# Tile offsets in on-chip memory and an earlier split of the mixed tokens, in a one-layer hybrid decoder trunk

## The chip, the cores and the metric

The kernel runs on one core of a Trainium2 chip. The metric is the device time of one execution in microseconds (us); the time of a kernel is the median of its runs. Before the change it is 2625.88 us, the median of 3 runs (2619.48 to 2629.32 us). The profile is taken from one further execution.

## The reference

One layer of a decoder trunk on 2048 tokens of width 1024, in float32. Cut to what matters:

```
mod = silu(c) @ w_ada + b_ada                      # shift, scale, gate for both sub-layers
h = rms(x) * norm_mix * (1 + scale1) + shift1
z = h @ w_in                                       # 1024 -> 3736 columns
mixed = concat(gla(...), hgrn2(...), mlstm(...))   # token mixers, chunk by chunk along the sequence
x = x + gate1 * (mixed @ w_out)                    # 1024 -> 1024
h = rms(x) * norm_mlp * (1 + scale2) + shift2
ff = relu(h @ w_ff1)**2 @ w_ff2                    # 1024 -> 4096 -> 1024
x = x + gate2 * ff
return rms(x) * final_norm
```

The three mixers are causal, so the mixing of a stretch of tokens needs the state that the stretch before it left. The dense products (`w_in`, `w_out`, `w_ff1`, `w_ff2`) have no order among token stretches.

## The kernel before, in words

**Quarters.** The tokens are cut into four quarters of 512 (`TQ`). All in-projections run first, quarter after quarter (`inproj`); then, for each quarter, the output projection (`outproj`), and the FFN (`f1` for `w_ff1`, `f2` for `w_ff2`) in six blocks of 5, 6, 6, 6, 5 and 4 hidden tiles (`NF`; `LB` is the last block's number).

**Dense products in three passes.** A float32 operand is split into a high part, rounded to the type `fp32r`, and a low part that holds the rest (`split`: ScalarE casts the high part, VectorE subtracts to get the low one). A product is the sum of three passes, high with high, high with low, low with high (`PASSES`). So each output tile of 128 x 512 over 1024 inputs is 8 x 3 = 24 matmuls. All go through the helper `mm` (line 165); `weights` (line 198) loads and splits a weight tile. Matmuls of the mixers go through `mm_late` (line 180) and `tr_late` (line 184) in plain float32.

**Pools.** On-chip memory is filled from both ends. From the left: constants, and the pool `wp`, with the ring of 15 split activation tiles (`ht`, 4,096 bytes a partition), raw weights (`raw`), split weights (`wt`), work tiles (`m5`). From the right: `m1`, the mixers' tiles, some of them small. When all mixing is done, `m1` is closed and the pool `lp` takes its place for the last quarter: split mixed tokens (`mt`, in pairs), split FFN inputs (`h2_0` to `h2_7`, shown as `h`), raw tiles, and the last block's split `w_ff2` weights. Tile sizes are rounded up to 32 bytes. A pool's base follows from all that was allocated ahead of it.

**Operands.** In the in-projection of most column groups the activation is the stationary operand and 384, 408 or 512 weight columns stream (`part`, line 834); two slices of 128 input rows lie behind one another in a weight tile. The 408 columns are group `q`. In `outproj`, `f1` and `f2` the weights are stationary and 512 tokens stream; in `f2_last`, at the very end, 256 tokens.

**Order.** The order on each engine is planned ahead from program order: a piece under `ahead()` counts as some 60 instructions earlier. Slots of a ring go to its tiles in the order of their first writes. Mixing is fed in between dense products: `pump` (line 1117) is called after every few matmuls and spends credit on steps of the block passes (pairs of positions within 16 tokens, on VectorE) and of the mixing chunks (four for each quarter); `finish(q)` (line 1131) emits at once whatever is left of quarter q's mixing; `prog.hold` stops mixing steps, not block passes, while the mixers' buffers are lent out.

**Around the change.** At the end of a quarter's FFN, ahead of the last `f2`, the main loop calls `finish(q + 1)`, and `outproj_in` (line 928) loads quarter q + 1's mixed tokens from device memory into mixing tiles lent for it (`spare`: `X`, `tm`, `v`) by POOL's DMA queue and splits them into eight ring tiles. `outproj` sets `prog.hold`, and `ffn_in` clears it when the FFN inputs are made. In `f1` the product is followed by its evacuation under `ahead()`: ReLU, square (which first writes the hidden tile), square, subtraction. This happens at the end of quarters 0 and 1; the last quarter's output projection comes earlier, within quarter 2, from `lp`.

Of the kernel before, what the change touches and what calls it, by code (L numbers as in the profile page):

```python
# [14 lines left out]
P = 128  # L15
# [86 lines left out]
def trunk(ctx, tc, I, out):  # L102
# [19 lines left out]
        return pm[0].tile([P, 1024], F32, tag="psm", name=name)  # L122


    mpx, ipx = ExitStack(), ExitStack()
    mpool = lambda name, bufs: mpx.enter_context(tc.tile_pool(name=name, bufs=bufs, side="right"))
    m1 = mpool("m1", 1)
# [67 lines left out]

    nraw, raw3 = [0], [ipool]

    def weights(src, n, lp=None):

        with ahead():  # L200
            nraw[0] += 1
            if raw3 and nraw[0] % 3 == 0 and n <= 816:
                raw = raw3[0].tile([P, 816], F32, tag="raw3", name="raw", bufs=1)
            else:
                raw = wp.tile([P, 1024], F32, tag="raw", name="raw", bufs=2)
            r = raw[:, 0:n]
            dma(out=r, in_=src)
            wt = (lp or wp).tile([P, 2, 1024], F32R, tag="wt", name="wt", bufs=4 if lp else 3)
            split(wt[:, 0, 0:n], wt[:, 1, 0:n], r)
        return wt[:, :, 0:n]  # L210

    def ring():
        return wp.tile([P, 2, TQ], F32R, tag="ht", name="ht", bufs=15)
# [89 lines left out]
    SH = m1.tile([P, 3, 128], F32, name="SH")  # L303
    SG3 = m1.tile([P, 256], F32, name="SG3")
    SG4 = m1.tile([P, 128], F32, name="SG4")
    SC = m1.tile([P, 2, 130], F32, name="SC")
    zero = m1.tile([P, 384], mybir.dt.bfloat16, name="zero")
    vaug = m1.tile([P, 4, 65], F32, name="vaug")
    mcar = m1.tile([4, 1], F32, name="mcar")
    Sd = m1.tile([P, 784], F32, name="Sd")  # L310
    for t_ in (SH, SG3, SG4, SC, zero, mcar, Sd):
        G.memset(t_, 0.0)
# [31 lines left out]
    def gates(q):  # L344

        g = gm[q % 3]
        li, y = g[:, 0, :], g[:, 1, :]
        w = lambda n, c=128: m1.tile([P, c], F32, tag="g_" + n, name="g_" + n)
        al, mt, b, be, lf, sm = w("al"), w("mt", 129), w("b"), w("be"), w("lf"), w("sm", 6)
        last = A.activation(out=al, in_=y, func=AF.Abs)  # L350
        V.tensor_scalar(out=lf, in0=y, scalar1=0.0, scalar2=None, op0=ALU.min)
        with ln_exp(last):
            A.activation(out=al, in_=al, func=AF.Exp, scale=-1.0)
            last = A.activation(out=al, in_=al, func=AF.Ln, bias=1.0)
        V.tensor_tensor(out=lf, in0=lf, in1=al, op=ALU.subtract)
        V.tensor_tensor_scan(out=b, data0=ones, data1=lf, initial=0.0, op0=ALU.mult, op1=ALU.add)
        V.memset(mt, 0.0)
        for n in range(4):
            r = slice(32 * n, 32 * n + 4)
            V.tensor_copy(out=mt[r, 0:1], in_=mcar if n == 0 else mt[32 * n - 32:32 * n - 28, 128:129])  # L360
            V.tensor_tensor_scan(out=mt[r, 1:129], data0=lf[r, :], data1=li[r, :], initial=mt[r, 0:1],
                                 op0=ALU.add, op1=ALU.max)
        V.tensor_copy(out=mcar, in_=mt[96:100, 128:129])
        yield
        V.tensor_tensor(out=al, in0=b, in1=mt[:, 1:129], op=ALU.subtract)
        V.tensor_tensor(out=be, in0=li, in1=b, op=ALU.subtract)
        for n in range(4):
            dma_m(out=R.al[q][n], in_=al[32 * n:32 * n + 4, :])
        ps = pt("ps_g")
        burst()  # L370
        tr = lambda i, t: tr_late(out=ps[:, 128 * i:128 * i + 128], in_=t, identity=ident)
        tr(0, be)
        V.tensor_tensor(out=sm[:, 0:1], in0=b[:, 127:128], in1=mt[:, 128:129], op=ALU.subtract)
        V.tensor_tensor(out=sm[:, 1:2], in0=sm[:, 0:1], in1=mt[:, 0:1], op=ALU.add)
        with ln_exp(last):
            A.activation(out=al, in_=al, func=AF.Exp, bias=mt[:, 0:1])
            A.activation(out=b, in_=mt[:, 1:129], func=AF.Exp, scale=-1.0)
            A.activation(out=lf, in_=be, func=AF.Exp, bias=sm[:, 0:1])
            A.activation(out=sm[:, 1:2], in_=sm[:, 1:2], func=AF.Exp)
        V.tensor_scalar(out=lf, in0=lf, scalar1=0.125, scalar2=None, op0=ALU.mult)  # L380
        V.tensor_scalar(out=sm[:, 2:6], in0=cst[:, 648:652], scalar1=sm[:, 1:2], scalar2=None, op0=ALU.mult)
        yield
        burst()
        for i, t in ((1, al), (2, b), (3, lf)):
            tr(i, t)
        gT = m1.tile([P, 4, 4, 4], F32, tag="gT", name="gT", bufs=2)
        V.tensor_copy(out=gT, in_=ps.rearrange("p (i n x) -> p i n x", i=4, n=4)[:, :, :, 0:4])
        ps = pt("ps_sc")
        burst()
        for pr in range(2):  # L390
            mm_late(ps[:, 4 * pr:4 * pr + 4], cst[:, 392 + 128 * pr:520 + 128 * pr], sm[:, 2:6], True, True)
        sc = m1.tile([P, 2, 4], F32, tag="sc", name="sc", bufs=2)
        V.tensor_copy(out=sc, in_=ps[:, 0:8].rearrange("p (a c) -> p a c", a=2))
        R.gT, R.sc = gT, sc
        yield
# [30 lines left out]
    def chunk(q, n, L, N):  # L426
# [120 lines left out]
        with hold:  # L547
            for pr in range(2):
                mm_late(psx_[:, pr, 260:390], L.qk[:, pr, :], SC[:, pr, :], True, True)
            for h in range(4):  # L550
                mm_late(psv[:, 65 * h:65 * h + 65], pe[:, h, :], vaug[:, h, :], True, True)
        hi_ = m1.tile([P, 4, 65], F32, tag="hi_", name="hi_")
        V.tensor_tensor(out=hi_.rearrange("p (a h) c -> p a h c", a=2),
                        in0=psx_[:, :, 260:390].rearrange("p a (h c) -> p a h c", c=65),
                        in1=gT[1].rearrange("p (a h) -> p a h", a=2)[:, :, :, None].to_broadcast([P, 2, 2, 65]),
# [7 lines left out]
        yield  # L563
        nxt(load_qk)
        nxt(load_al)
        st = m1.tile([P, 56], F32, tag="st40", name="st40")
        den, mu, ss, rs = st[:, 0:4], st[:, 4:8], st[:, 8:24], st[:, 24:40]
        V.scalar_tensor_tensor(out=den, in0=hi_[:, :, 64], scalar=-1.0, in1=hi_[:, :, 64],
                               op0=ALU.mult, op1=ALU.max)
# [201 lines left out]
    def inproj(q, hts, nxt):  # L771
# [62 lines left out]
        def part(g, c0, n, ps, kk):  # L834

            kind = GROUPS[g][0]
            w = weights(I[f"wg{g}"][:, 2 * kk:2 * kk + 2, c0:c0 + n], 2 * n).rearrange("p a (k n) -> p a k n", k=2)
            for ti in range(len(ps)):
                for k2 in range(2):
                    k = 2 * kk + k2  # L840
# [87 lines left out]
    def outproj_in(q, lp=None):  # L928
        mt = []
        if lp is None:  # L930
            raws = spare(SPARE_Z, lambda c: R.zx[q][:, c, :])
        for c in range(KT):
            if lp is None:
                raw = raws[c]
# [54 lines left out]
                yield  # L989
        prog.hold = False  # L990

    def f1(h2, ft):
        w = weights(I["w1"][ft].rearrange("p c n -> p (c n)"), 1024)
        hd = ring()
        ps = psd.tile([P, 512], F32, tag="psd", name="ps_f1")
        for k in range(KT):
            for i, (a, b) in enumerate(PASSES):
                mm(ps, w[:, b, 128 * k:128 * k + 128], h2[k][:, a], k == 0 and i == 0, k == KT - 1 and i == 2)
            if k % 2:
                pump(1.3)  # L1000
        with ahead():
            r = m5()
            A.activation(out=r, in_=ps, func=AF.Relu)  # L1003
# [189 lines left out]
        pass  # L1193
    tail = iter(())
    for q in range(NQ):
        hds = []
        for ft in range(NF[0]):
            hds.append(f1(h2, ft))
            next(tail, None)
# [4 lines left out]
        for b in range(LB):  # L1204
# [5 lines left out]
            next(steps, None)  # L1210
            f2(hds, b, acc, steps)
            for i in range(1, NF[b + 1]):
                nh.append(f1(h2, F0[b + 1] + i))
                next(steps, None)
            hds = nh
            if q == NQ - 2 and b == EARLY:
                finish(NQ - 1)
                mpx.close()
                lp = ctx.enter_context(tc.tile_pool(name="lp", bufs=1, side="right"))
                sm1 = outproj(NQ - 1, outproj_in(NQ - 1, lp), lp)  # L1220
        if q == NQ - 1:
# [1 line left out]
            break  # L1223
        steps = iter(())
        if q < NQ - 2:
            finish(q + 1)
            h2n = []
            steps = ffn_in(h2n, q + 1, *outproj(q + 1, outproj_in(q + 1)))
        f2(hds, LB, acc, steps)
        h2 = h2n  # L1230
        tail = final_steps(q, acc)
# [34 lines left out]
```

## Time and profile before

| | |
|---|---|
| median of 3 runs | 2625.88 us (2619.48 to 2629.32) |
| profiled execution | 2632.36 us, span 2630.3 us |
| TensorE, matmuls | 2545.6 us busy, 97% |
| TensorE, weight loads | 2177.5 us, 83% |
| VectorE | 1787.1 us, 68% |
| ScalarE | 1232.5 us, 47% |
| GpSimd | 259.9 us, 10% |
| mean granted clock of TensorE | 0.989 |

How to read it: busy times are sums over the whole span and do not say which engine a stage waits for; for that, views by stage, by group and by wait are shown with the prediction. Each line names the engine, the source line, the operation, and the tiles as written <- read. PE is TensorE's matmuls, PEld its weight loads (they run beside the matmuls), DVE is VectorE, ACT ScalarE, POOL GpSimd, SP the queue that issues most DMAs. Matmuls are pipelined and their ends are modelled, so the distance between starts says more than a duration. The digits of tile names are left out: `h2_0` to `h2_7` appear as `h`, `ps_f1` and `ps_f2` both as `ps_f`.

### The profile page before, as it was taken

How to read it: one execution, taken by the hardware profiler on the slowest of the kernel's cores; microseconds unless marked ns; L12 is line 12 of the kernel's file. 1: busy time of each engine (PE TensorE's matmuls, PEld its weight loads, DVE VectorE, ACT ScalarE, POOL GpSimd, SP SyncE). 2: the span in 40 equal slices, each digit the busy share in tenths (PEclk: the TensorE clock that was granted, in tenths of full speed). 3: DMA queues.
4: the chain of work that ended last, by engine and by line, in shares of the span. 5: the costliest groups of instructions: out<-in, count | busy, mean ns of one | idle time of the engine just before them, and what ended most of it. 6: DMA issues, size and time to landing. Idle time of an engine off the chain costs nothing. (4 is left out here: it accounts for less than half of the span.)

```text
span 2630.3 us, 39618 instructions
## 1 busy us (share of the span) xinstructions
PE 2545.6 (97%) x15050; PEld 2177.5 (83%) x15050; DVE 1787.1 (68%) x3344; ACT 1232.5 (47%) x2191; POOL 259.9 (10%) x435
## 2 busy tenths in 40 slices
PE   5899999999999999999999999999999999999998
PEld 5889888899888788888878888888888888888887
DVE  8785786987975978876887666547566645533335
ACT  4654455545643634554453545445445543433333
POOL 0101102021102112112110000100000010000000
PEclk9999999999999999999999999999999999999999
DMA  8777676586457345446464343444433254433332
GB/s 266 211 222 218 180 216 189 170 243 198 144 143 234 107 113 146 138 142 166 128 184 135 125 131 116 146 133 161 131 123 119 88 181 148 141 114 93 94 96 80
DMA packets 160199, 401.75 MB, mean 153 GB/s; under 512 B 20473, under 2 KB 60490, under 8 KB 160010
## 3 DMA queue, kind: packets, MB, share of 16 engines
q1 hardware_dynamic: 129338, 306.51, 37.3%
q0 software_dynamic: 30672, 92.73, 12.7%
q8 instruction: 118, 1.93, 0.3%
q14 instruction: 71, 0.58, 0.1%
HBM read 336.21 MB, written 62.95 MB: 152 GB/s over the span
## 5 line engine op out<-in xcount | busy, mean ns | idle before, releaser
L165 PE MATMUL ps_f<-ht,wt 128*128 128x512 f32 (+1 forms) x5472 | 1252.3, 388 | 5.6 <-ACT ht L225 5.5
L165 PEld LDWEIGHTS ps_f<-ht,wt 128*128 128x128 f32 x5472 | 1008.8, 188 | 213.4 <-ACT ht L225 6.1
L194 DVE TENSOR_TENSOR wt<-raw,wt 128x1024 fp32r<-128x1024 f32 (+3 forms) x436 | 499.1, 1146 | 431.3 <-ACT wt L193 429.6
L193 ACT CAST wt<-raw 128x1024 fp32r<-128x1024 f32 (+3 forms) x436 | 431.6, 991 | 665.2 <-PE ps_f L165 345.4
L165 PE MATMUL ps_ip<-wt,ht 128*128 128x384 f32 (+2 forms) x3072 | 593.6, 352 | 29.4 <-ACT st L823 8.6
L165 PEld LDWEIGHTS ps_ip<-wt,ht 128*128 128x128 f32 x3072 | 554.6, 193 | 56.2 <-ACT st L823 10.6
L1023 DVE SCALAR_TENSOR_TENSOR acc<-ps_f,mod,acc 128x512 f32<-128x512 f32 (+1 forms) x200 | 145.1, 727 | 106.0 <-PE ps_f L165 105.3
L1003 ACT ACTIVATE m<-ps_f 128x512 f32<-128x512 f32 x128 | 76.9, 601 | 288.4 <-PE ps_f L165 288.2
L165 PE MATMUL ps_f<-h,wt 128*128 128x512 f32 x768 | 181.4, 397 | 0.0
L165 PEld LDWEIGHTS ps_f<-h,wt 128*128 128x128 f32 x768 | 144.6, 188 | 35.6 <-issue 0.5
L165 PE MATMUL ps_op<-ht,wt 128*128 128x512 f32 x576 | 133.1, 393 | 3.8 <-ACT ht L193 3.8
L165 PEld LDWEIGHTS ps_op<-ht,wt 128*128 128x128 f32 x576 | 109.0, 190 | 26.9 <-ACT ht L193 3.9
L323 POOL DMA_DIRECT2D blk<-zq x144 | 93.6, 661 | 353.0 <-DVE prod L333 169.4
L333 DVE TENSOR_TENSOR prod<-blk 128x768 f32<-128x768 f32 (+3 forms) x192 | 111.1, 578 | 2.6
L334 DVE TENSOR_REDUCE Sd<-prod 128x48 f32<-128x768 f32 (+3 forms) x192 | 110.5, 576 | 2.9
L1006 DVE TENSOR_TENSOR ht<-m,ht 128x512 fp32r<-128x512 f32 x128 | 88.2, 689 | 22.3 <-ACT m L1005 22.2
L332 DVE TENSOR_TENSOR blk<-blk 128x720 f32<-128x720 f32 (+4 forms) x180 | 98.9, 550 | 1.6 <-DMA blk<-zq 1.4
L165 PE MATMUL ps_ip<-ht,wt 128*128 128x512 f32 x384 | 100.0, 410 | 0.0
L165 PEld LDWEIGHTS ps_ip<-ht,wt 128*128 128x128 f32 x384 | 73.2, 196 | 15.6 <-issue 1.4
L1005 ACT ACTIVATE m<-m 128x512 f32<-128x512 f32 x128 | 81.1, 634 | 2.8
L1004 ACT ACTIVATE ht<-m 128x512 fp32r<-128x512 f32 x128 | 81.3, 635 | 0.1
L189 ACT ACT_TABLE_LOAD x57 | 73.1, 1283 | 1.0
(390 smaller groups left out, 2355.7 us busy)
## 6 DMA issues: line engine op xcount, KB each, us to landing
raw<-w SPq DMA_DIRECT2D x256, 512.0 KB, 3.5
raw<-wg SPq DMA_DIRECT2D x100, 384.0 KB, 4.0
m<-wada SPq DMA_DIRECT2D x64, 256.0 KB, 3.9
raw<-wo SPq DMA_DIRECT2D x32, 512.0 KB, 3.6
m<-xq SPq DMA_DIRECT2D x56, 256.0 KB, 3.5
raw<-wg SPq DMA_DIRECT2D x28, 512.0 KB, 5.0
blk<-zq POOLq DMA_DIRECT2D x144, 96.0 KB, 6.7
zt<-zq POOLq DMA_DIRECT2D x48, 288.0 KB, 4.4
```

The source lines that it names most:

```text
L165: T.matmul(out=ps, lhsT=l, rhs=r, start=start, stop=stop)
L193: A.copy(out=hi, in_=src)
L194: V.tensor_tensor(out=lo, in0=src, in1=hi.bitcast(F32), op=ALU.subtract)
L323: dma_m(out=t[i][32 * g:32 * g + 32], in_=src)
L332: V.tensor_tensor(out=t[1][:, 0:n, :], in0=t[1][:, 0:n, :], in1=t[2][:, d:16, :], op=ALU.mult)
L333: V.tensor_tensor(out=prod[:, 0:n, :], in0=t[1][:, 0:n, :], in1=t[0][:, d:16, :], op=ALU.mult)
L334: V.tensor_reduce(out=s49[:, 0:n, d:d + 33:16], in_=prod[:, 0:n, :].rearrange("p j (u c) -> p j u c", c=16), op=ALU.add, axis=AX.X)
L1003: A.activation(out=r, in_=ps, func=AF.Relu)
L1004: A.activation(out=hd[:, 0], in_=r, func=AF.Square)
L1005: A.activation(out=r, in_=r, func=AF.Square)
L1006: V.tensor_tensor(out=hd[:, 1], in0=r, in1=hd[:, 0].bitcast(F32), op=ALU.subtract)
L1023: V.scalar_tensor_tensor(out=acc[:, dt, c], in0=ps, scalar=mod[:, 40 + dt:41 + dt], in1=acc[:, dt, c], op0=ALU.mult, op1=ALU.add)
```

## The change

It has four parts.

1. A tile of 32 bytes (`top`) is allocated at the right edge ahead of the mixers' pool, and one of 128 bytes (`gap`) ahead of `lp`. Nothing reads or writes them; they move what comes after.
2. `weights` takes a number of blocks, `ks`. The in-projection passes 2, and the second block then starts at the next multiple of 128 columns. This differs from before for group `q` alone (408 columns, block 2 now at column 512).
3. Eight small tags of the mixers' pool are allocated in multiples of 64 bytes and used through a view of the old shape.
4. In quarters 0 and 1, `finish(q + 1)`, the hold on mixing and `outproj_in(q + 1)` move ahead: the first two to just before the last `f1` of the quarter, the loads and splits to between that `f1`'s matmuls and its evacuation.

```diff
+    ctx.enter_context(tc.tile_pool(name="top", bufs=1, side="right")).tile([P, 8], F32, name="top")
     mpx, ipx = ExitStack(), ExitStack()
...
-    def weights(src, n, lp=None):
+    def weights(src, n, lp=None, ks=1):
...
-            split(wt[:, 0, 0:n], wt[:, 1, 0:n], r)
-        return wt[:, :, 0:n]
+            if ks == 1:
+                split(wt[:, 0, 0:n], wt[:, 1, 0:n], r)
+                return wt[:, :, 0:n]
+            m = n // ks
+            wv = wt[:, :, 0:ks * ((m + 127) // 128 * 128)].rearrange("p a (k s) -> p a k s", k=ks)[:, :, :, 0:m]
+            split(wv[:, 0], wv[:, 1], r.rearrange("p (k s) -> p k s", k=ks))
+        return wv
...
-    SC = m1.tile([P, 2, 130], F32, name="SC")
+    SC = m1.tile([P, 272], F32, name="SC")[:, 0:260].rearrange("p (a c) -> p a c", a=2)
-    vaug = m1.tile([P, 4, 65], F32, name="vaug")
-    mcar = m1.tile([4, 1], F32, name="mcar")
+    vaug = m1.tile([P, 272], F32, name="vaug")[:, 0:260].rearrange("p (h c) -> p h c", h=4)
+    mcar = m1.tile([4, 16], F32, name="mcar")[:, 0:1]
...
-        w = lambda n, c=128: m1.tile([P, c], F32, tag="g_" + n, name="g_" + n)
+        w = lambda n, c=128: m1.tile([P, (c + 15) // 16 * 16], F32, tag="g_" + n, name="g_" + n)[:, 0:c]
...
-        sc = m1.tile([P, 2, 4], F32, tag="sc", name="sc", bufs=2)
+        sc = m1.tile([P, 16], F32, tag="sc", name="sc", bufs=2)[:, 0:8].rearrange("p (a c) -> p a c", a=2)
...
-        hi_ = m1.tile([P, 4, 65], F32, tag="hi_", name="hi_")
+        hi_ = m1.tile([P, 272], F32, tag="hi_", name="hi_")[:, 0:260].rearrange("p (h c) -> p h c", h=4)
...
-        st = m1.tile([P, 56], F32, tag="st40", name="st40")
+        st = m1.tile([P, 64], F32, tag="st40", name="st40")
...
-            w = weights(I[f"wg{g}"][:, 2 * kk:2 * kk + 2, c0:c0 + n], 2 * n).rearrange("p a (k n) -> p a k n", k=2)
+            w = weights(I[f"wg{g}"][:, 2 * kk:2 * kk + 2, c0:c0 + n], 2 * n, ks=2)
...
             raws = spare(SPARE_Z, lambda c: R.zx[q][:, c, :])
+        prog.hold = lp is None and q > 0
...
-    def f1(h2, ft):
+    def f1(h2, ft, before=None):
...
+        if before:
+            before()
         with ahead():
             r = m5()
...
-        hds = []
+        hds, mts = [], []
...
-                nh.append(f1(h2, F0[b + 1] + i))
+                early = q < NQ - 2 and b == LB - 1 and i == NF[LB] - 1
+                if early:
+                    finish(q + 1)
+                    prog.hold = True
+                nh.append(f1(h2, F0[b + 1] + i, (lambda: mts.extend(outproj_in(q + 1))) if early else None))
...
+                ctx.enter_context(tc.tile_pool(name="gap", bufs=1, side="right")).tile([P, 32], F32, name="gap")
                 lp = ctx.enter_context(tc.tile_pool(name="lp", bufs=1, side="right"))
...
-            finish(q + 1)
             h2n = []
-            steps = ffn_in(h2n, q + 1, *outproj(q + 1, outproj_in(q + 1)))
+            steps = ffn_in(h2n, q + 1, *outproj(q + 1, mts))
```

## The prediction

> **What bounds the kernel now.** I read the page first, then busy time by stage, then TensorE's timeline by start times, because matmul ends are modelled.
>
> ```profile
> span 2630.3 us, 39618 instructions
> PE 2545.6 (97%) x15050; PEld 2177.5 (83%) x15050; DVE 1787.1 (68%) x3344; ACT 1232.5 (47%) x2191; POOL 259.9 (10%) x435
> 100.00:900.00 800.00, 763.55 (x4707) 698.36 (x4706) 615.26 (x1198) 410.54 (x741) 107.08 (x173) 0.98 0.64 190
> 1250.00:1300.00 50.00, 48.12 (x210) 39.61 (x210) 44.59 (x75) 26.69 (x44) 1.12 (x2) 0.97 0.37 117
> 1760.00:2100.00 340.00, 339.47 (x2304) 281.45 (x2303) 219.39 (x432) 166.26 (x314) 19.39 (x33) 1.00 0.40 127
> 2144.00:2190.00 46.00, 46.00 (x198) 37.02 (x197) 19.70 (x23) 14.13 (x19) 2.15 (x4) 1.00 0.64 207
> 2400.00:2596.00 196.00, 195.96 (x856) 159.82 (x854) 74.41 (x79) 69.67 (x94) 0.00 (x0) 1.00 0.31 96
> ```
>
> The stage rows give PE, PEld, DVE, ACT, POOL, then granted clock, DMA share and GB/s. From 900 us on TensorE is idle for a few us only. There, time changes only if a matmul gets shorter or one of the few idle gaps goes. The input projection (100 to 900) loses 36 us to waits, so an ns saved there may be swallowed by one.
>
> **Part 1: the last quarter's tiles.** In the rows below (start, length, group), `ht` are tiles of the left pool, `h` and `mt` those of `lp`, the last quarter's own pool at the right edge; all weights `wt` here are on the left.
>
> ```profile
> 2144.45 45.14 PE L165 MATMUL ps_op<-mt,wt 128*128 128x512 f32 x192
> 2189.43 5.61 PE L165 MATMUL ps_f<-ht,wt 128*128 128x512 f32 x24
> ...
> 2323.07 33.89 PE L165 MATMUL ps_f<-h,wt 128*128 128x512 f32 x144
> 2356.80 32.83 PE L165 MATMUL ps_f<-ht,wt 128*128 128x512 f32 x144
> 2389.47 10.70 PE L165 MATMUL ps_f<-h,wt 128*128 128x512 f32 x45
> ```
>
> Start to start, 144 products on `h` take 33.73 us, 234.2 ns each; 144 on `ht` take 32.67 us, 226.9 ns each; 192 on `mt` take 44.98 us, 234.3 ns each. Same shape, full clock, no wait: 7.3 to 7.4 ns apart. Summing tile sizes in order of allocation (32-byte steps), all left tiles that these products read start 320 bytes past a multiple of 512, and the tiles of `lp` 480 past one: its 77,824 bytes are 152 times 512 and end at an edge that is 480 past. The change puts 32 bytes (`top`) and 128 bytes (`gap`) ahead of it: 480 - 160 = 320. If the offset is the cause, 768 products on `h` and 192 on `mt` fall to 226.9 ns: 768 x 7.3 + 192 x 7.4 = **7.0 us**, all on the path (PE 195.96 of 196.00 us). The other end is 0, if something else about `lp` is slow; I take 7.0, since width, weights and clock agree and the two kinds alternate within one stretch.
>
> [...]
>
> The last 192 products, 256 wide, read weights from `lp` and `ht` from the left.
>
> ```profile
> 2595.95 13.41 PE L165 MATMUL ps_f<-ht,wt 128*128 128x256 f32 x109
> 414.82 5.02 PE L165 MATMUL ps_ip<-wt,ht 128*128 128x384 f32 x28
> 420.88 2.69 PE L165 MATMUL ps_ip<-wt,ht 128*128 128x408 f32 x13 [1.04 <-ACT st L802]
> 424.01 14.74 PE L165 MATMUL ps_ip<-wt,ht 128*128 128x408 f32 x76 [0.44 <-DVE wt L194]
> ```
>
> A group's last matmul outlasts its slot by some 0.16 us (33.89 against 33.73 above). Less that, the first row gives 121.6 ns each. The 384-wide row gives 173.2 by the same working; with 226.9 for 512 that is 0.42 ns a column, hence 119.5 for 256. At most 192 x 2.1 = 0.4 us is there to gain; I take 0.
>
> **Part 2: group q.** Its weights lie as two blocks of 408 columns; the second starts 1,632 bytes in, 96 past a multiple of 512. The change puts it 2,048 in. The 384- and 512-wide groups stay where they were. 192 of the 384 products are touched. At 7.4 ns they give 1.4 us; the last row shows 191.7 ns where the line through 384 and 512 says 183.3, so at the most 384 x 8.4 = 3.2 us; at the least 0, because waits such as the 1.04 us above absorb it. I take half of 1.4, **0.7 us**. The split writes the same elements through a two-block pattern: costed at nothing, under TensorE's work; DVE and ACT are at 77% and 51% of that stage.
>
> **Part 3: small tiles padded to 64 bytes.** These feed mixing alone. Bound: 7.3 of 226.9 is 3.2%, on the mixing matmuls' busy time of 261.7 us (192.39 + 69.26 below): 8.4 us either way.
>
> ```profile
> sum 2010.00, PE 192.39; mean PE 96.19
> sum 2010.00, PE 69.26; mean PE 34.63
> 1885.21 1.73 PE ps_m L180 x16
> 1909.35 3.73 PE ps_oo L180 x32
> ```
>
> The first two sum lines 180 and 184, from 100 to 900 and 900 to 2110. I take 0: by the last two, mixing products of 64 to 130 columns take 108 to 117 ns whatever their width, so something other than streaming paces them.
>
> **Part 4: the early split.** It concerns the output projections of quarters 1 and 2; the second one:
>
> ```profile
> PE ps_op L165 <- ACT ht L193: 3.8, 2, 1.9
> L922 POOL DMA_DIRECT2D spare<-zx x24: 544/560/586, 789.6 to 1697.6; - x24
> L193 ACT CAST ht<-spare x24: 607/620/625, 795.0 to 1740.4; 128x512 fp32r<-128x512 f32 x24
> L194 DVE TENSOR_TENSOR ht<-spare,ht x24: 682/684/693, 795.6 to 1741.9; 128x512 fp32r<-128x512 f32 x24
> 1734.28 0.60 ACT L1003 ACTIVATE m<-ps_f 128x512 f32<-128x512 f32 x1 [2.71 <-PE ps_f L165]
> 1734.77 1.04 ACT L193 CAST wt<-raw 128x1024 fp32r<-128x1024 f32 x1
> 1735.70 0.63 ACT L1004 ACTIVATE ht<-m 128x512 fp32r<-128x512 f32 x1
> 1736.23 0.61 ACT L193 CAST ht<-spare 128x512 fp32r<-128x512 f32 x1
> 1736.90 9.44 PE L165 MATMUL ps_op<-ht,wt 128*128 128x512 f32 x40 [1.88 <-ACT ht L193]
> ```
>
> The mixed tokens were being loaded from 1697.6 us at the latest, 38 us before use, yet the first cast stands behind the last FFN tile's ReLU (1734.28) and square (1735.70): ring slots go out in the order of first writes, and that square comes first. The change emits loads and splits ahead of them. Moved at each boundary: 8 loads (8 x 0.56 = 4.5 us on POOL's queue, where they already run 38 us ahead; behind them on POOL are the next quarter's mixing loads, which wait for these buffers and get them one FFN tile sooner), 8 casts (5.0 us of ACT), 8 subtractions (5.5 us of DVE). Nothing of it is on SP's queue. Of the ring's 15 slots 11 are taken then (8 of `h2`, 3 finished FFN tiles), so four split tiles find a slot at once and the rest take those that the last FFN tile's products give back, one each 0.68 us. The tile they move into lasts 5.45 us; ACT has the 2.71 us above free in it, so some 2.3 us of casts spill past its end and the ReLU and squares wait that long behind them; who needs these is the block after the projection, some 44 us on. Each product needs a new split tile only every 3 x 0.227 = 0.68 us, casts take 0.62: the projection need not wait. Also behind the casts is the next weight's cast (1734.77), not wanted until the second output tile, 5.4 us on. Gain **3.8 us**; least 0, if DVE, 89% busy in 1250 to 1300, delivers the low halves late.
>
> One gap is followed by a slow clock:
>
> ```profile
> 1274.17 16.21 PE L165 MATMUL ps_op<-ht,wt 128*128 128x512 f32 x63 [1.88 <-ACT ht L193]
> 1275.30:1278.70 3.40, 3.40 (x10) 0.50 0.47 154
> 1720.00:1760.00 40.00, 38.12 (x172) 31.38 (x171) 20.91 (x32) 21.06 (x36) 1.07 (x2) 1.00 0.41 133
> ```
>
> For 3.4 us the granted clock was 0.50: 1.7 us lost. The other gap, equally long, lost none. I take half, **0.85 us**.
>
> [...]
>
> **Sum.** 7.0 + 0.7 + 3.8 + 0.85 = 12.4 us. The profiled execution took 2632.4 us (2.1 around its span), 6.5 over the median of the runs, and had the clock drop in full: 2632.4 - 13.2 = 2619.2. Off the median, 2625.9 - 12.4 = **2613.5 us**.
>
> **Rivals.**
> - *The offset is not the cause.* Then something else about `lp` costs the 7.3 ns, its place at the far end of the memory for instance, which the change leaves. Parts 1 and 2 give 0: 2625.9 - 4.65 = 2621. For: addresses stand in no view. Against: the alternating rows, and the 408-wide row, slow without any tile of `lp`. 0.08. [...]
> - *The wait changes hands.* ACT is free earlier but TensorE then waits as long for DVE's low halves or a weight: parts 1 and 2 remain, 2618. For: DVE at 89%. Against: at the second boundary DVE is 52% busy (20.91 of 40 us). 0.12.
> - *Mixing gains too.* If mixing products pay the same 3.2% for their 32-byte offsets, padding saves up to 8.4 us more: 2605 at the lowest. For: both kinds read two tiles at once. Against: their pace does not follow their width. 0.14.
> - *Slower: the mixing backlog.* Mixing is now held from one FFN tile earlier (5.2 us of the planner's time) in quarters 0 and 1. If that leaves a chunk undone when the last quarter's tokens are demanded, `finish` emits it uncovered: a quarter of the planner's 85.6 us, 21.4 us, and the kernel takes 2635. It decides once the delay, 10.4 us, exceeds the cover. The last mixing product at 2109.10 ends 34 us before the projection at 2144.45:
>
> ```profile
> 2109.10 1.03 PE L184 MATMUL ps_x<-cst,mx 128*128 128x128 f32 x8
> 1683.93 1.06 PE L184 MATMUL ps_x<-cst,mx 128*128 128x128 f32 x8 [0.30 <-DVE mx L680]
> ```
>
> Cover 34 against 10.4; ahead of the second boundary it is 50 us (1683.93 to 1734.28). 0.05.
>
> **How the numbers follow.** My forecast has the remaining 0.61. Its own range: 7.0 + 1.9 = 8.9 to 7.4 + 1.4 + 3.8 + 1.7 = 14.3 us off, 2617 to 2611.6, and some 3 us for executions that lie between 2619.5 and 2629.3. The cases at 2605, 2618 and 2621 widen it to 2604 to 2623, leaving out the slow one and little more. A measurement of this kernel tells about 0.5%, 13.1 us, from no change; the forecast, at 0.47%, sits just inside. A little under half of its 0.61 and nearly all of the mixing case fall beyond 2612.7: faster 0.42. Slower 0.05. Same 0.53.
>
> **What would show it.** Right: starts of `h` and `mt` products 227 ns apart; no wait of `ps_op` for ACT's `ht`; the casts ahead of the ReLU; clock 1.00 at both boundaries. Wrong: 234 ns again (offset); a `ps_op` wait on DVE or weights (early split); mixing products close ahead of 2144 us (backlog); mixing sums other than 192 and 69 us (small tiles).

## The result

| kernel | median | runs |
|---|---|---|
| before | 2627.60 us | 6, from 2619.48 to 2633.78 us |
| after | 2608.97 us | 6, from 2608.05 to 2611.37 us |

The ratio is 0.993 with a 95% interval of 0.9912 to 0.9949: 18.4 us faster, 13 to 23. Here and below, microseconds of a timed gain are the ratio's distance from 1 times the median of before. The runs of after also lie closer together, within 3.3 us where those of before spread over 14. One execution of `q_blocks`, a kernel of the next section, took 3162.49 us at a granted clock of 0.75; its ratio leaves it out, and the median of its other 11 runs is 2623.78 us.

The page of after, its span, its busy times and three groups of part 5 (group, count | busy us, mean ns | idle us before them and what ended it):

```profile
span 2607.2 us, 39620 instructions
PE 2533.9 (97%) x15050; PEld 2175.2 (83%) x15050; DVE 1786.1 (69%) x3344; ACT 1231.5 (47%) x2191; POOL 259.5 (10%) x435
L167 PE MATMUL ps_f<-h,wt 128*128 128x512 f32 x768 | 175.7, 390 | 0.0
L167 PE MATMUL ps_op<-ht,wt 128*128 128x512 f32 x576 | 131.1, 389 | 0.0
...
blk<-zq POOLq DMA_DIRECT2D x144, 96.0 KB, 5.9
```

Two of these groups in the profile of before:

```profile
L165 PE MATMUL ps_f<-h,wt 128*128 128x512 f32 x768 | 181.4, 397 | 0.0
L165 PE MATMUL ps_op<-ht,wt 128*128 128x512 f32 x576 | 133.1, 393 | 3.8 <-ACT ht L193 3.8
```

The profiled execution is 23 us shorter than that of before (2607.2 against 2630.3). Lines have moved on (165 is now 167, 193 is 195, 1003 is 1015). The three rows of after answer to three parts of the change: products on `h` lost 5.7 us of busy time, the output projections have no idle time before them any more (3.8 us before), and the loads of `blk` land after 5.9 us (6.7 before).

Busy time by stage of after, with the columns of the prediction's table; the stages from 2126 on answer to those from 2144 on of before:

```profile
100.00:900.00 800.00, 771.30 (x4747) 706.13 (x4746) 623.80 (x1227) 418.56 (x755) 106.95 (x173) 0.98 0.64 191
1250.00:1300.00 50.00, 50.00 (x223) 41.39 (x222) 45.57 (x76) 24.88 (x42) 7.67 (x13) 1.00 0.51 155
1760.00:2100.00 340.00, 339.84 (x2314) 281.85 (x2313) 222.40 (x443) 170.96 (x334) 20.26 (x34) 1.00 0.40 125
2126.00:2172.00 46.00, 46.00 (x205) 38.09 (x204) 20.19 (x24) 13.93 (x19) 2.15 (x4) 1.00 0.66 208
2400.00:2575.00 175.00, 174.96 (x785) 145.27 (x784) 68.78 (x75) 59.51 (x79) 0.00 (x0) 1.00 0.31 97
```

Two things stand out. From 1250 to 1300 TensorE is never idle and its clock is 1.00 (48.12 us and 0.97 before). And from 100 to 900 it is busy for 7.8 us more than before, in the in-projection, for which the prediction had almost nothing. By itself that is no proof: in the trace of `lp_offset`, which changes nothing there, it is 769.28 us, 5.7 more than in this one of before.

To see where the 23 us come from, the table below takes the starts of the same dense matmul in each profiled execution and subtracts the start in the profile of before. The matmuls are named by their time in before; 828 is near the end of the in-projection, 1251 and 1509 lie around the first early split, 1779 and 2058 after the second, and 2618 is the last one.

```
start in before, us    828     971    1251    1509    1779    2058    2618
after                -10.3    -9.6    -9.7   -13.3   -16.4   -15.8   -23.1
lp_offset            -10.1   -10.1   -10.1   -11.9   -10.4   -10.5   -17.8
q_blocks              -4.9    -4.4    -4.5    -6.1    -6.2    -6.2    -6.2
small_tiles          -15.3   -14.3   -14.4   -15.4   -15.4   -15.5   -15.5
early_split           -3.8    -2.7    -2.8    -6.0    -9.1    -8.3    -8.4
left_480             -11.1   -11.1   -11.2   -11.9   -10.5   -10.6   -17.9
blk_aligned          -10.7   -10.2   -10.2   -11.2   -11.2   -11.3   -11.4
```

Behind 971 us a column tells a part of the change to a few tenths, but for steps of some 1.6 us where one of the two executions has a drop of the clock and the other has none (`lp_offset` gains one by 1509 us and loses one by 1779): 6.1 us from 1251 to 2058 for the early split, 7.3 us from 2058 on for `lp`. Up to 828 us single executions scatter: every kernel is ahead of this one execution of before by 4 to 15 us, those too that change nothing there (`lp_offset`, `left_480`). What the in-projection gained is therefore taken from timed runs, and from averages over many traces. The six rows below after are the kernels of the next section.

### The profile page after: what moved, and what is told of

Read it like the earlier page. It is cut to its first block, busy times and chain, and to the rows that moved or that the text cites. A ratio compares the mean times of both kernels' runs of the same rounds, so it can differ in the third digit from the quotient of the medians.

```text
span 2607.2 us, 39620 instructions
## 1 busy us (share of the span) xinstructions
PE 2533.9 (97%) x15050; PEld 2175.2 (83%) x15050; DVE 1786.1 (69%) x3344; ACT 1231.5 (47%) x2191; POOL 259.5 (10%) x435
## 3 DMA queue, kind: packets, MB, share of 16 engines
q0 software_dynamic: 30672, 92.73, 12.6%
## 5 line engine op out<-in xcount | busy, mean ns | idle before, releaser
L167 PE MATMUL ps_f<-h,wt 128*128 128x512 f32 x768 | 175.7, 390 | 0.0
```

The source lines that it names most:

```text
L167: T.matmul(out=ps, lhsT=l, rhs=r, start=start, stop=stop)
```

## The experiments

Every timed kernel was compared with runs of before made on the same chip in the same session.

### Each part alone

`lp_offset` is before with the last quarter's pool moved, and nothing else:

```diff
+                ctx.enter_context(tc.tile_pool(name="gap", bufs=1, side="right")).tile([P, 40], F32, name="gap")
                 lp = ctx.enter_context(tc.tile_pool(name="lp", bufs=1, side="right"))
```

> The kernel before with one edit: 160 bytes left free ahead of the last quarter's pool, so that its tiles start 320 instead of 480 bytes past a multiple of 512; the mixers' tiles stay. If the offset makes the 7.3 ns (the prediction's part 1): products on h and mt at 227 ns, the kernel 7.0 us faster, all of it after 2144 us. If something else about that pool does (its place): 234 ns still, 0 us.

Measured: 2618.92 us, ratio 0.997 (0.9954 to 0.9986), 7.9 us faster. In the trace 7.3 us of it fall after 2058 us. First the timeline of after, then that of `lp_offset`, with products on `h` and `ht` in turn:

```profile
2304.74 32.80 PE L167 MATMUL ps_f<-h,wt 128*128 128x512 f32 x144
2337.38 32.80 PE L167 MATMUL ps_f<-ht,wt 128*128 128x512 f32 x144
2370.02 30.31 PE L167 MATMUL ps_f<-h,wt 128*128 128x512 f32 x133
```

```profile
2310.05 32.80 PE L165 MATMUL ps_f<-h,wt 128*128 128x512 f32 x144
2342.69 32.80 PE L165 MATMUL ps_f<-ht,wt 128*128 128x512 f32 x144
2375.33 32.80 PE L165 MATMUL ps_f<-h,wt 128*128 128x512 f32 x144
```

All stretches of 144 products take 32.64 us from start to start, 226.7 ns each, where those on `h` took 33.73 us before. 160 bytes of place are worth 7 us.

`q_blocks` is before with part 2 alone:

```diff
-            w = weights(I[f"wg{g}"][:, 2 * kk:2 * kk + 2, c0:c0 + n], 2 * n).rearrange("p a (k n) -> p a k n", k=2)
+            w = weights(I[f"wg{g}"][:, 2 * kk:2 * kk + 2, c0:c0 + n], 2 * n, ks=2)
...
```

> The kernel before with group q's second weight block moved to column 512, nothing else. The prediction's part 2: 0.7 us faster, within 0 to 3.2. The rival, after the traces of both kernels showed some 10 us less in the input projection: this is the part that does it, 6 to 10 us faster, with shorter waits of ps_ip.

Measured: 2624.22 us, ratio 0.9992 (0.9979 to 1.0005); not to be told from no change. The same 30 products in the timeline of before, then of `q_blocks`:

```profile
640.87 5.86 PE L165 MATMUL ps_ip<-wt,ht 128*128 128x408 f32 x30 [0.31 <-ACT st L802]
```

```profile
642.09 5.81 PE L165 MATMUL ps_ip<-wt,ht 128*128 128x408 f32 x30 [0.32 <-ACT st L807]
```

0.05 us over 30 products is 1.7 ns each, and 0.6 us over all 384. All 408-wide products of a trace say more (distances over 230 ns, which hold a wait, left out): in before the mean distance of starts is 185.4 ns on the first block and 187.1 on the second, in `q_blocks` 184.8 and 185.0. So the second block was the slower one and no longer is, by 2.1 ns on 192 products, 0.4 us.

`small_tiles` is before with part 3 alone: `top`, the eight padded tags, and a `gap` of 480 bytes that leaves `lp` at its old offset of 480:

```diff
+    ctx.enter_context(tc.tile_pool(name="top", bufs=1, side="right")).tile([P, 8], F32, name="top")
...
-    SC = m1.tile([P, 2, 130], F32, name="SC")
+    SC = m1.tile([P, 272], F32, name="SC")[:, 0:260].rearrange("p (a c) -> p a c", a=2)
...
+                ctx.enter_context(tc.tile_pool(name="gap", bufs=1, side="right")).tile([P, 120], F32, name="gap")
```

> The kernel before with the small mixing tiles padded to 64 bytes and the mixers' pool moved by 32, the last quarter's pool kept at 480. The prediction's part 3: 0 us, bounds 8.4 either way by TensorE. The rival: the tiles that the block passes load in pieces of 192 bytes now start at multiples of 64, their loads land sooner (6.7 to 5.9 us in the traces of the two kernels), the input projection's stores and so its evacuations wait less, 5 to 9 us faster, all of it before 880 us, and the runs lie closer together.

Measured: 2621.97 us, ratio 0.9977 (0.9964 to 0.9991), 6.0 us faster. Mixing goes on until 2058 us, but after 971 us the column stands still, from -14.3 to -15.5: the mixing matmuls gain nothing, and what the timed runs gain must lie in the in-projection. The runs do not lie closer together, against what was expected: 12 of them spread over 15.5 us. What changed is in the row of the `blk` loads, before and then `small_tiles`:

```profile
blk<-zq POOLq DMA_DIRECT2D x144, 96.0 KB, 6.7
```

```profile
blk<-zq POOLq DMA_DIRECT2D x144, 96.0 KB, 6.1
```

`early_split` is before with part 4 alone, the diff of its fourth part as it stands above.

> The kernel before with the early split alone. The prediction's part 4: the two waits of 1.9 us of ps_op for ACT gone, 3.8 us faster, and up to 1.7 more where the slow clock after the first gap goes with it. The rival that the wait changes hands: a wait of ps_op for DVE or for a weight, 0 us.

Measured: 2618.89 us, ratio 0.9972 (0.996 to 0.9984), 7.4 us faster, 4 to 11. In the trace 5.6 us of it (-2.8 to -8.4) lie after 1251 us, at the two boundaries, 3.2 (a drop of the clock in before among them) and 3.1 at the one and the other, less 0.7 given back.

Together the four ratios give 7.9 + 2.1 + 6.0 + 7.4 = 23.4 us; the joint change gives 18.4, and its interval ends at 23. Each of the four has an interval of 3 us or more to either side, so nothing shows that the parts hinder one another, nor that they help.

### What of part 3 makes the gain

Part 3 does two things. By the sum of tile sizes, most tiles of the mixers' pool in before, `blk` among them, start 32 bytes past a multiple of 64, and a few (`SH`, `SC`) at one. `top` turns that round, and padding brings the few to a multiple too. Two kernels do one each, with `lp` at 480 in both. `moved_not_padded` has `top` alone, so that `blk` starts at a multiple of 64:

```diff
+    ctx.enter_context(tc.tile_pool(name="top", bufs=1, side="right")).tile([P, 8], F32, name="top")
...
+                ctx.enter_context(tc.tile_pool(name="gap", bufs=1, side="right")).tile([P, 120], F32, name="gap")
```

> The kernel before with the mixers' pool moved by 32 bytes and nothing padded: the tiles that DMAs fill (blk, zt, v, gate and so on) now start at multiples of 64, the small ones SH, SG3, SG4, SC do not; the last quarter's pool stays at 480. If the start of the tiles that DMAs fill is what small_tiles gained by: 3 to 8 us faster, blk loads landing in 6.1 us or less. If the padding of the small tiles is: 0 us, blk loads at 6.5 to 6.7.

`padded_not_moved` has the padding alone, so that all of the pool's tiles start 32 past a multiple of 64:

```diff
-    SC = m1.tile([P, 2, 130], F32, name="SC")
+    SC = m1.tile([P, 272], F32, name="SC")[:, 0:260].rearrange("p (a c) -> p a c", a=2)
...
```

> The counterpart: the eight small tags padded to 64 bytes, the pool not moved, so that every mixing tile starts 32 bytes past a multiple of 64. If the start of the tiles that DMAs fill counts: 0 us, blk loads at 6.5 to 6.7 us. If the padding counts: 3 to 8 us faster.

`after_moved_32` is the kernel after with the mixers' pool moved by 32 bytes, `lp` kept at 320:

```diff
-    ctx.enter_context(tc.tile_pool(name="top", bufs=1, side="right")).tile([P, 8], F32, name="top")
+    ctx.enter_context(tc.tile_pool(name="top", bufs=1, side="right")).tile([P, 16], F32, name="top")
...
-                ctx.enter_context(tc.tile_pool(name="gap", bufs=1, side="right")).tile([P, 32], F32, name="gap")
+                ctx.enter_context(tc.tile_pool(name="gap", bufs=1, side="right")).tile([P, 24], F32, name="gap")
```

> The changed kernel with the mixers' pool moved by another 32 bytes, so that all its tiles start 32 past a multiple of 64; the last quarter's pool is kept at 320. If the start counts: 11 to 15 us faster than before instead of 18, blk loads at 6.5 us or more, runs further apart than the changed kernel's 3.3 us. If not: 18 us, as the changed kernel.

Measured: `moved_not_padded` 2620.14 us, ratio 0.9984 (0.997 to 0.9997); `padded_not_moved` 2626.32 us, ratio 1.0005 (0.9992 to 1.0018); `after_moved_32` 2612.09 us, ratio 0.9952 (0.9935 to 0.9969), 12.6 us faster than before instead of 18.4 (the two intervals meet, 0.9935 to 0.9969 and 0.9912 to 0.9949). By these three it is the place that counts, and padding by itself does nothing that could be measured.

Two more kernels ask which tiles. `blk_aligned` is before with the three `blk` tiles alone used from a multiple of 64, and `blk_off` is after with these alone used from 32 past one. The edit is the same in both, a view that begins 32 bytes into a wider tile:

```diff
-            t.append(m1.tile([P, 16, 48], F32, tag="blk", name="blk", bufs=3))
+            t.append(m1.tile([P, 784], F32, tag="blk", name="blk", bufs=3)[:, 8:776].rearrange("p (a c) -> p a c", a=16))
```

> The kernel before, in which the blk tiles alone are used from a multiple of 64 bytes (a view that begins 32 bytes into a wider tile); everything else keeps its place, 32 past one. If the start of blk is enough: loads land in 5.7 to 6.1 us and the kernel is 4 to 6 us faster, ratio 0.998. If it needs the other tiles too, or the gain has another source: within 1.5 us of before.

> The kernel after the change, in which the three tiles that the block passes load (blk, 144 loads in pieces of 192 bytes) alone are used from 32 bytes past a multiple of 64; everything else keeps its place. If the start of these tiles is what part 3 gained by: their loads land in 6.4 to 6.7 us again instead of 5.9, and 4 to 6 us of the 18 come back, 2613 to 2615 us. If the gain lies in another tile (zt, v, gate, SH, SC) or in what VectorE reads: within 1.5 us of the kernel after, 2609 us, and VectorE's products on blk keep their 953 ns either way.

Measured: `blk_aligned` 2620.90 us, ratio 0.9974 (0.9962 to 0.9987), 6.8 us faster than before. `blk_off` 2616.49 us, ratio 0.9956 (0.994 to 0.9971), 11.6 us faster than before where after is 18.4; its six runs, 2613.91 to 2619.22 us, all lie above the six of after. So one tag of three tiles, the target of 144 loads, carries as much as part 3 gains in all: 6.8 us (3 to 10) put into before, 6.8 taken out of after, 6.0 (2 to 9) for part 3.

The loads run in pieces of 192 bytes (16 runs of 48 floats a partition). The page's landing time tells the two sorts apart only roughly: 5.7 to 6.1 us where `blk` starts at a multiple of 64, 6.2 to 6.7 where it does not, but 6.0 in `blk_off`, against what was expected. The time of the single packets on POOL's queue is clearer; the table has its packets of 1,920 and 4,224 bytes, 3,072 of each size. Together they hold 18.87 MB, which is what the 144 loads of `blk` and the 48 stores of `sd` move in pieces of 192 bytes, at 96 KB each.

```
                   blk starts    1,920 bytes    4,224 bytes   mean ns of a packet
before             32 past 64          156.5          324.0
padded_not_moved   32 past 64          156.0          314.4
after_moved_32     32 past 64          157.3          323.5
blk_off            32 past 64          151.9          316.7
blk_aligned        0                   140.7          296.9
moved_not_padded   0                   134.4          292.0
small_tiles        0                   139.9          295.1
after              0                   140.4          301.9
```

The worst of the four below is better than the best of the four above, and the six traces that the table leaves out fall the same way (153.8 to 156.3 and 318.9 to 324.3 ns in the four with `blk` 32 past, 137.0 to 141.0 and 294.0 to 295.5 in the two with it at a multiple): some 16 and 27 ns a packet between before and `blk_aligned`, on 3,072 each 132 us of DMA engine time, or 8 us on each of 16 engines. Why a packet takes longer at the one place than at the other, no run shows.

VectorE reads these tiles no faster (before, then `blk_aligned`); only its wait for the load is shorter:

```profile
L333 DVE TENSOR_TENSOR prod<-blk 128x768 f32<-128x768 f32 x7 | 6.7, 952 | 0.0
L332 DVE TENSOR_TENSOR blk<-blk 128x720 f32<-128x720 f32 x7 | 6.3, 902 | 1.4 <-DMA blk<-zq 1.4
```

```profile
L333 DVE TENSOR_TENSOR prod<-blk 128x768 f32<-128x768 f32 x7 | 6.7, 952 | 0.0
L332 DVE TENSOR_TENSOR blk<-blk 128x720 f32<-128x720 f32 x7 | 6.3, 901 | 0.5 <-DMA blk<-zq 0.5
```

That TensorE gets on faster by it shows over all 14 traces: from 100 to 900 us it is busy for 763.6 to 769.7 us in the eight with `blk` 32 past a multiple of 64 and for 768.0 to 771.7 us in the six with it at one, 766.7 and 770.3 on the average. How it gets there is not settled. A way that the waits from 100 to 900 us allow is the in-projection's own stores: ScalarE waits for a `zv` store to free a buffer, and TensorE for ScalarE. The waits (total us, times, longest) of before and of `blk_aligned`:

```profile
ACT st L823 <- DMA zv<-st: 17.7, 7, 7.5
PE ps_ip L165 <- ACT st L823: 8.6, 6, 4.4
```

```profile
ACT st L823 <- DMA zv<-st: 14.1, 5, 5.4
PE ps_ip L165 <- ACT st L823: 6.4, 4, 3.1
```

After against `blk_off` goes the same way (6.8 against 7.2 us for TensorE). But 2 us are not 6, and single traces scatter too much: `padded_not_moved`, no faster than before in its runs, has 14.8 us of the first wait, and `lp_offset`, which leaves `blk` where it was, has 14.6 and 6.4 us, much like `blk_aligned`. Over all 14 traces TensorE's waits for ScalarE's `st` are 10.8 us on the average with `blk` 32 past and 8.5 with it at a multiple, some 2 of the 3.7 us. The way is argued, not shown.

### What about the offset makes products slow

The prediction gave the cost to operands that start differently modulo 512 bytes; 480 might also be a bad place in itself. `left_480` is before with 160 bytes at the very left, so that the left tiles too are at 480:

```diff
+    cp.tile([P, 40], F32, name="pad")
```

> The kernel before with 160 bytes left free at the very left: all tiles of the left pools start 480 past a multiple of 512, as those of the last quarter's pool do. If only the difference of the two offsets counts (part 1): h and mt products at 227 ns, ht products at 227 too, 7 us less after 2144 us. If the offset 320 itself is fast and 480 slow: 234 ns everywhere, 60 us slower. The input projection's tiles st move to 32 past a multiple of 64, so it may lose what small_tiles gained.

Measured: 2617.91 us, ratio 0.9964 (0.995 to 0.9977), 9.5 us faster; the loss in the in-projection that was thought possible is not to be seen beside the 7.9 us of `lp_offset`. Its timeline, `h` at 480 and `ht` at 480:

```profile
2309.95 32.80 PE L166 MATMUL ps_f<-h,wt 128*128 128x512 f32 x144
2342.59 32.80 PE L166 MATMUL ps_f<-ht,wt 128*128 128x512 f32 x144
2375.23 25.10 PE L166 MATMUL ps_f<-h,wt 128*128 128x512 f32 x110
```

32.64 us for each 144 again. Nothing is wrong with 480, nor with `lp`'s place at the far end; what counts is the difference between the moving tile and the weights. Two single executions ask which differences cost. `lp_352` is after with `lp` at 352, 32 past the left tiles:

```diff
-                ctx.enter_context(tc.tile_pool(name="gap", bufs=1, side="right")).tile([P, 32], F32, name="gap")
+                ctx.enter_context(tc.tile_pool(name="gap", bufs=1, side="right")).tile([P, 24], F32, name="gap")
```

> The kernel after the change with lp 32 bytes further, at 352 where the left tiles are at 320: the smallest difference that allocation allows. If only equality counts: 234 ns on h and mt, 7 us more than the kernel after. If the cost goes by the distance or by 64 bytes: 227 to 228 ns, nothing lost.

`steps_64` is after with 64 bytes between the eight `h` tiles:

```diff
+            if lp is not None and k:
+                lp.tile([P, 16], F32, name=f"step{k}")
             h2.append(ring() if lp is None else lp.tile([P, 2, TQ], F32R, name=f"h2_{k}"))
```

> The kernel after the change, with 64 bytes between the eight h tiles of the last quarter, so that they start 64, 128, 192, 256, 320, 384, 448 and 0 bytes (modulo 512) past the left tiles' offset; mt and the last weights start 64 past it. If only equality counts: products on seven of the eight tiles are 234 ns apart, on the eighth 227; 672 products x 7.3 ns and 192 x 7.4 give 6.3 us more than the kernel after. If the cost grows with the distance: small next to 0, largest at 256. If it is a matter of the value modulo 64 or 128: tiles at 128, 256 and 384, or all eight, are as quick as the eighth.

Measured: 2618.99 and 2611.55 us, one execution each. The timeline of `lp_352`, then of `steps_64`:

```profile
2132.34 44.97 PE L167 MATMUL ps_op<-mt,wt 128*128 128x512 f32 x192
2177.14 5.64 PE L167 MATMUL ps_f<-ht,wt 128*128 128x512 f32 x24
...
2310.69 33.77 PE L167 MATMUL ps_f<-h,wt 128*128 128x512 f32 x144
2344.29 32.84 PE L167 MATMUL ps_f<-ht,wt 128*128 128x512 f32 x144
```

```profile
2126.92 44.13 PE L167 MATMUL ps_op<-mt,wt 128*128 128x512 f32 x192
2170.89 5.65 PE L167 MATMUL ps_f<-ht,wt 128*128 128x512 f32 x24
...
2304.23 33.54 PE L167 MATMUL ps_f<-h,wt 128*128 128x512 f32 x144
2337.61 32.81 PE L167 MATMUL ps_f<-ht,wt 128*128 128x512 f32 x144
```

At 32 bytes of difference the products are 33.60 / 144 = 233.3 ns apart, nearly the full price. With `mt` 64 bytes off they are 43.97 / 192 = 229.0 ns apart, under a third of it. So distance is not the measure, nor equality alone. In `steps_64` the eight `h` tiles, by the mean distance from their 96 products to the next one (one distance of 642 ns behind `h_0` left out):

```
past the weights, bytes     64    128    192    256    320    384    448      0
tile                       h_0    h_1    h_2    h_3    h_4    h_5    h_6    h_7
ns                       233.1  232.7  232.2  230.0  232.8  232.2  231.7  230.1
its three passes         232.6  232.2  229.7  225.9  231.8  232.4  228.4  225.8
                         233.7  234.3  233.7  235.6  233.3  232.6  233.3  235.8
                         233.1  231.7  233.3  228.5  233.4  231.6  233.3  228.6
```

Tiles four apart, 256 bytes, agree: the tile at 256 takes the same 226, 236 and 229 ns in its passes as the one with no difference. None of the three expectations holds: the pattern repeats after 256 bytes, so that 256 is as good as 0 here. And even the tile at 0 isn't at 226.7 ns, since its second pass takes 236. So a product's neighbours seem to count as well: 64 bytes cost `mt`, where all products have them, 2.3 ns, and `h_0` 6.4. What in the hardware does this stays open, and so does a kernel with every tile 256 apart, which wasn't run.

## Why the prediction came out as it did

The median fell by 18.4 us, where the forecast had 12.4 and 2613.5 us; 2608.97 lies inside its range of 2604 to 2623, but outside the 2617 to 2611.6 us that the forecast had for itself: it is in the part that was added for the mixing case. The 18.4 us are past the 13.1 us that it could not tell from no change, where it had given "faster" 0.42. That the total fell inside is partly luck, since the gain that widened the range came another way. By its parts:

**Part 1, the last quarter's tiles: right, cause and size.** 7.0 us predicted, 7.3 in the traces of after and of `lp_offset`, and 7.9 (3.7 to 12) in the timed runs. The rival that the offset is not the cause falls with `lp_offset` and `left_480`, which move different tiles and end the same. The distance of products went from 234.2 (before) to 226.7 ns (`lp_offset`) with nothing changed but where the moving tiles lie, so in this kernel the places of moving tile and weights bear on each other; what in the hardware does that, no run shows. The last 192 products, 256 wide, had their weights in `lp` and are 120.8 ns apart in before and in after alike: nothing was to be gained there, as the prediction took it.

**Part 2, group q: right in the cause, right in size by luck.** 0.7 us predicted, 0.4 to 0.6 by the products above; the runs can't tell it from nothing. The prediction had 7.4 ns a product and halved the sum for waits that might absorb it; the products on the second block gained 2.1 ns. Its upper bound rested on one row of 191.7 ns, where the mean of before is 186.

**Part 3, small tiles: the step that failed.** It costed the padding at nothing because "these feed mixing alone", and argued only about TensorE: mixing products whose pace does not follow their width. On that it was right. The sums of the mixing products of after, lines 182 and 186, are as before:

```profile
sum 2010.00, PE 192.50 PEld 171.34; mean PE 96.25 PEld 85.67
sum 2010.00, PE 69.97 PEld 57.26; mean PE 34.98 PEld 28.63
```

192.50 and 69.97 us against 192.39 and 69.26. But the same tiles are filled by DMAs, and `top`, which the prediction noticed only as a shift of `lp`, also shifted them to multiples of 64. That is worth 6.0 us alone, 6.8 with `blk` only. So the rival "mixing gains too" has about the right amount and the wrong mechanism, and its chance of 0.14 was argued about the wrong engine. The prediction noted that the in-projection loses 36 us to waits, but drew from it only that an ns saved on TensorE "may be swallowed"; it did not ask which of its own changes would touch the transfers in that stage.

**Part 4, the early split: right in mechanism, the clock's term too small.** Both waits of `ps_op` for ACT's `ht` are gone, and no wait on VectorE or on a weight took their place; the rival that the wait changes hands falls. The timeline of after at the first boundary (ScalarE, VectorE, TensorE in order of start):

```profile
1258.36 0.61 ACT L195 CAST ht<-spare 128x512 fp32r<-128x512 f32 x1
...
1259.40 2.69 ACT L195 CAST ht<-spare 128x512 fp32r<-128x512 f32 x5
...
1260.53 4.30 DVE L196 TENSOR_TENSOR ht<-spare,ht 128x512 fp32r<-128x512 f32 x7
...
1261.64 10.59 PE L167 MATMUL ps_op<-ht,wt 128*128 128x512 f32 x46
1261.99 0.59 ACT L1015 ACTIVATE m<-ps_f 128x512 f32<-128x512 f32 x1
1262.48 1.14 ACT L195 CAST ht<-spare 128x512 fp32r<-128x512 f32 x2
1263.51 0.64 ACT L1016 ACTIVATE ht<-m 128x512 fp32r<-128x512 f32 x1
```

Six of the eight casts run ahead of the last tile's ReLU (1261.99) and the other two ahead of its square (1263.51), 1.1 us where the prediction had 2.3 us of casts in the way of these; the projection starts at 1261.64 with no idle time. The sum was 3.8 + 0.85 = 4.65 us, or 5.5 against the profiled execution, whose clock drop was in full; its trace gives 6.1 net and `early_split` alone 5.6. The timed 7.4 (4 to 11) holds all of these.

The prediction took half a drop of the clock, 0.85 us, for the two gaps together. It should have been a whole one. Eight profiles keep the two gaps of 1.88 us: before, `lp_offset`, `q_blocks`, `small_tiles`, `moved_not_padded`, `padded_not_moved`, `left_480` and `blk_aligned`. Behind their 16 gaps the clock fell to 0.50 for 3.4 us 8 times. The timeline's row for the first boundary of `left_480`, then its clock there (last columns: clock, DMA share, GB/s), then the row of `blk_aligned`, without a drop:

```profile
1263.00 45.45 PE L166 MATMUL ps_op<-ht,wt 128*128 128x512 f32 x192 [1.88 <-ACT ht L194]
```

```profile
1264.40:1267.80 3.40, 3.40 (x10) 0.50 0.38 146
```

```profile
1264.02 43.83 PE L165 MATMUL ps_op<-ht,wt 128*128 128x512 f32 x192 [1.88 <-ACT ht L193]
```

45.45 less 43.83 is 1.6 us a drop, and 8 drops in eight executions make 1.6 us for each: 5.4 us with the two gaps, where the traces have 5.6 and 6.1. In the six profiles with the split moved there is none at the 12 boundaries. In the traces the drop goes with the place of the gap. In each of the 14 the starts and ends of all stretches at 0.50 between 60 and 2500 us lie on one grid of 3.413 us, to within 2 ns, so that the cells of this grid can be laid over the gaps. In before the first gap, 1272.29 to 1274.17 us, lies wholly in the cell from 1271.92 to 1275.33, and the clock is at 0.50 from 1275.33 on; the second, 1735.02 to 1736.90, is cut at 1736.13 into 1.11 and 0.77 us, and no drop follows. Over the 16, one cell held 1.71 to 1.88 us of the gap ahead of each of the 8 drops; of the 8 gaps without a drop, seven were cut by the grid so that no cell held more than 1.41 us, and one had 1.79 us in one cell. So a drop followed 8 of the 9 gaps with 1.71 us or more in one cell, and none of the others; why the ninth had none, no trace shows. An estimate from the two lengths measured here: a gap of 1.88 us that falls anywhere on the grid lies wholly in one cell of 3.413 us in (3.413 - 1.88) / 3.413 = 45% of cases, which goes with 8 drops in 16.

**The mixing backlog** did not come. The last mixing product of after ends 34 us ahead of the projection at 2128.65 us, and the stage from 1760 to 2100 has 339.84 us of 340 busy:

```profile
2093.30 1.03 PE L186 MATMUL ps_x<-cst,mx 128*128 128x128 f32 x8
```

**The spread** is still open: after's runs lie within 3.3 us where before's lie within 14. Two waits that cost 1.6 us more in some executions and not in others are gone, which accounts for up to 3.2 of it. But `after_moved_32`, with the early split too, spreads over 10.7 us and `small_tiles` over 15.5; the rest was not traced.

## What to carry to other kernels

Where an engine seems to slow down on some tiles of the same shape, compare start addresses: pools that fill memory from both ends get offsets by accident, and 160 bytes of dummy tiles were worth 0.3% here. Ask of every tile that moves who else touches it, the DMAs that fill it too, and not only the engine that the change is about. And a short wait ahead of a dense stretch is dearer than its length when the clock may drop behind it: 1.88 us cost 2.7 on the average of 16 here.

## What the runs showed of the hardware

- Dense products of 512 columns run 226.7 ns apart when the moving tile and the weights start at the same offset modulo 512 (by the sum of tile sizes), 233.3 when they are 32 bytes apart, 229.0 at 64 and 234.2 at 160 (32 and 64 in one execution each); tiles 64 bytes from one to the next repeat their pattern after 256 bytes (233.1, 232.7, 232.2 and 230.0 ns from 64 to 256, then 232.8, 232.2, 231.7 and 230.1, in one execution). At 408 columns a difference of 96 bytes costs 2.1 ns (187.1 against 185.0), at 256 columns one of 160 bytes nothing (120.8 with it and without).
- Packets of the queue with the loads in pieces of 192 bytes take 9 to 11% longer (156.5 against 140.7 ns, 324.0 against 296.9) when the loads' target starts 32 bytes past a multiple of 64 instead of at one.
- A gap of 1.88 us on TensorE is followed by 3.4 us at a granted clock of 0.50 in 8 of 16 cases, in all of which 1.71 us or more of it lie in one cell of a grid of 3.413 us, as 1.79 us do in one of the 8 others.
